# Moving the hi and lo weight tiles, and the activation pairs, to other SBUF addresses

## The chip, the cores and the metric

One core of one Trainium2 chip runs the kernel. The metric is the device time of one execution in microseconds (us), the median of several runs.

## The reference, cut to what matters

One decoder layer for 256 tokens of width 2048, then a final RMSNorm. All inputs are float32.

```
h = h + W_out[ concat( NSA(8 heads), StickBreaking(8 heads) ) ]
h = h + MemoryCrossAttention(rmsnorm(h), rmsnorm(mem))
h = h + PEER(rmsnorm(h))        # s = x U^T for experts, gelu, times V, top-k gated
y = rmsnorm(h)
...
a = jnp.einsum('td,ted->te', xb, u_tab[eb])
hidden = gb.astype(xb.dtype) * jax.nn.gelu(a)
return jnp.einsum('te,ted->td', hidden, v_tab[eb])
```

PEER has 16384 experts, so `u_tab` and `v_tab` have 16384 rows of 2048 numbers each. The kernel computes `x U^T` for all experts, 128 at a time, and multiplies with those rows of V that some token chose.

## The kernel before, in words

Every large product is made with float32r operands in three passes, so that it is nearly as exact as float32. A number is split into `hi` (rounded to float32r by ScalarE) and `lo` (what is left, by VectorE). Of activations both halves lie side by side in a "pair" tile: columns 0 to 255 of a block are the high part of 256 tokens, columns 256 to 511 the low part.

Weights come in pieces of 128x1024 numbers. `raw` (L63) loads a piece through SP's queue into one of four buffers, `parts` (L75) has ScalarE write one of three `hi` buffers (L77) and VectorE one of three `lo` buffers (L79). `scaled` (L110) does the same for rows of V with a factor (L113, L115).

`fm_block` (L152) makes one block of 128 outputs x 256 tokens in two halves of eight 128x128 weight blocks. `fm_mm` (L126) is one half. It issues eight matmuls with a block of `hi` as the stationary operand and 512 columns of the pair as the moving one (L133), and then eight with a block of `lo` and 256 columns (L135). This form carries the projections, W_out (`pair_o`), the memory attention's products, the query product of PEER and all 128 blocks of U (`pair_f`): in all 398 halves, 3184 matmuls at L133 and as many at L135. Stationary blocks are 512 bytes apart in a partition, moving blocks 2048.

`tm_block` (L173) turns the roles round: a block of the pair is stationary, 512 columns of `hi` or `lo` move (L187, L188, L193). `fm_short` (L137) serves the memory attention's output with 256 columns at a time. In the V phase (`v_phase`, products at L1202) a tile of hidden values is stationary (`hh`, `hl`, or a 0/1 tile kept in a `listed` buffer), and 512 columns of `hi` or `lo` of gathered V rows move.

Two smaller products use float32r too. `gates` (L561) splits a 128x384 piece into `wgh` and `wgl` and uses stationary blocks of 24 columns, so 96 bytes apart. `compress` (L508) uses stationary blocks of 60 columns from a tile called `cmp`, 240 bytes apart, against 256 moving columns (L536). `whole_block` (L156) multiplies in plain float32, with the loaded piece as it is (L162).

Tiles get their addresses from pools that are opened one behind the other: constants, then `st` (four `raw`, three `hi`, three `lo`), then `pb` (`pair_x`, `pair_h`, `pair_f`, one after the other in one place), then the front's tiles `fp` (`pair_m`, `pair_o` and `cmp` in one place, `om`), later in its place PEER's `ba` (the gathered rows `hb` and `vrows`) and `gw` (`hh` and `hl`). In the kernel before, the byte address of every `raw`, `hi`, `lo`, pair, `hh` and `hl` is a multiple of 256 (10752 for the first `raw`, 27136 for the first `hi`, 39424 for the first `lo`, 51712 for `pair_f`, 84480 for `pair_o`). So every stationary and every moving operand of L133, L135, L187 to L193 and L1202 starts at the same place modulo 256.

The order of the work is set by the scheduler of the framework and by hand-written dependencies. The program is one stream on each engine, and no instruction reads an address at run time that the change moves, but for the gathers' lists.

Of the kernel before, what the change touches and what calls it, by code (L numbers as in the profile page):

```python
# [18 lines left out]
F32 = mybir.dt.float32  # L19
F32R = mybir.dt.float32r  # L20
# [10 lines left out]
KD = D // 128  # L31
# [3 lines left out]
NEG = -1e30  # L35
N_CMP = 15
HALF = 1024
RAW, HI, LO = 4, 3, 3
GROUP = 8
W = 258  # L40
# [13 lines left out]
class Layer:  # L54
# [18 lines left out]

    def parts(self, raw, eng=None):
        nc = self.nc  # L75
        hi = self.st.tile([128, HALF], F32R, tag="hi", name="hi", bufs=HI)
        self.last_hi = nc.scalar.activation(hi, raw, AF.Copy)  # L77
        lo = self.st.tile([128, HALF], F32R, tag="lo", name="lo", bufs=LO)
        self.last_lo = (eng or nc.vector).tensor_tensor(out=lo, in0=raw, in1=hi.bitcast(F32), op=ALU.subtract)  # L79
        self.pace.append(self.last_lo)  # L80
        self.held()
        return hi, lo

    def split_cut(self, src):

        nc = self.nc
        raw = self.st.tile([128, HALF], F32, tag="raw", name="raw", bufs=RAW)
        hi = self.st.tile([128, HALF], F32R, tag="hi", name="hi", bufs=HI)
        lo = self.st.tile([128, HALF], F32R, tag="lo", name="lo", bufs=LO)
        for n in range(2):  # L90
            cs = slice(n * 512, (n + 1) * 512)
            nc.sync.dma_start(raw[:, cs], src[:, cs])
            nc.scalar.activation(hi[:, cs], raw[:, cs], AF.Copy)
            nc.vector.tensor_tensor(out=lo[:, cs], in0=raw[:, cs], in1=hi[:, cs].bitcast(F32), op=ALU.subtract)
        return hi, lo
# [13 lines left out]

    def scaled(self, raw, val):  # L110
        nc = self.nc
        hi = self.st.tile([128, HALF], F32R, tag="hi", name="hi", bufs=HI)
        nc.scalar.activation(hi, raw, AF.Copy, scale=val)  # L113
        lo = self.st.tile([128, HALF], F32R, tag="lo", name="lo", bufs=LO)
        self.last_lo = nc.vector.scalar_tensor_tensor(lo, raw, val, hi.bitcast(F32), op0=ALU.mult, op1=ALU.subtract)  # L115
        self.held()
        return hi, lo
# [122 lines left out]
    def run(self):  # L240
        nc, tc, a = self.nc, self.tc, self.a
        with ExitStack() as top:
            enter = top.enter_context
            self.accs = ExitStack()
            self.accp = self.accs.enter_context(tc.tile_pool(name="accp", bufs=3, space=bass.MemoryType.PSUM))
            self.cst = enter(tc.tile_pool(name="cst", bufs=1))
            self.dram = enter(tc.tile_pool(name="dram", bufs=1, space=bass.MemoryType.DRAM))
            self.st = enter(tc.tile_pool(name="st", bufs=1))
            self.pb = enter(tc.tile_pool(name="pb", bufs=1))
            c = self.cst  # L250
            self.ident = c.tile([128, 128], F32, name="ident")
            self.iota = c.tile([128, 16], F32, name="iota")
            self.ones = c.tile([128, 128], F32, name="ones")
            self.gs = c.tile([128, 4, KD], F32, name="gs")
            self.rstd = c.tile([128, T], F32, name="rstd")
            self.rstd_c = c.tile([128, 16], F32, name="rstd_c")[:, :2]
            nc.gpsimd.dma_start(self.gs, a["gains"])
            nc.gpsimd.dma_start(self.ident, a["ident"])
            nc.gpsimd.dma_start(self.iota, a["iota"][:, :16])
            nc.vector.memset(self.ones, 1.0)  # L260
            self.hres = self.dram.tile([128, KD, T], F32, name="hres")
            self.rows = [self.dram.tile([n + (hi - lo) * 128, W], F32, name="rows%d" % part)
                         for part, (n, (lo, hi)) in enumerate(zip(ROWS, PARTS))]

            self.table = self.dram.tile([128 * 128 * T, 1], F32, name="table")
            self.by_key = self.table.rearrange("(j x) o -> j (x o)", j=128)
            self.front()
            self.peer()

    def front(self):  # L270
        nc, tc, a = self.nc, self.tc, self.a
        with ExitStack() as es:
            fp = es.enter_context(tc.tile_pool(name="fp", bufs=1))
            ps = es.enter_context(tc.tile_pool(name="fps", bufs=1, space=bass.MemoryType.PSUM))
            self.fp, self.ps = fp, ps
            pair = fp.tile([128, KD, 2 * T], F32R, tag="pair", name="pair_m")
            om = fp.tile([128, 4, 2 * T], F32R, tag="om", name="pair_om")
            self.vt = [fp.tile([128, T], F32, name=n) for n in ("norm_v", "norm_t")]
            self.vt2 = [fp.tile([128, 2], F32, name=n) for n in ("norm_v2", "norm_t2")]
            ssq = fp.tile([128, T], F32, tag="ssq", name="ssq_m")  # L280

            memT = fp.tile([128, KD, T], F32, tag="big", name="memT")
# [88 lines left out]
            for part in range(2):  # L371
                for r in range(0, ROWS[part], 7 * 128):
                    n = min(7, (ROWS[part] - r) // 128)
# [69 lines left out]
            for b2 in range(8):  # L443
                hi, lo = self.split(a["w_mem_o"][b2])
# [116 lines left out]
    def gates(self, xp):  # L561

        nc, a, fp = self.nc, self.a, self.fp
        src = fp.tile([128, KD * 24], F32, tag="l", name="wg", bufs=2)
        nc.sync.dma_start(src, a["w_gate"])
        hi = self.st.tile([128, HALF], F32R, tag="hi", name="wgh", bufs=HI)[:, :KD * 24]
        nc.scalar.activation(hi, src, AF.Copy)
        lo = self.st.tile([128, HALF], F32R, tag="lo", name="wgl", bufs=LO)[:, :KD * 24]
        nc.vector.tensor_tensor(out=lo, in0=src, in1=hi.bitcast(F32), op=ALU.subtract)
        p = self.acc([24, 2 * T])  # L570
        self.fm_mm(p, hi, lo, xp, range(KD), True, True, m=24)
        gT = fp.tile([24, T], F32, name="gT")
        self.join(p, gT)
        nc.vector.tensor_mul(gT, gT, self.rstd[:24, :])
        nc.scalar.activation(gT, gT, AF.Sigmoid)
        p = self.ps.tile([128, 2, 24], F32, tag="sm", name="ps_gt", bufs=1)
        for tb in range(2):
            nc.tensor.transpose(p[:, tb, :], gT[:, tb * 128:(tb + 1) * 128], self.ident[:24, :24])
        out = fp.tile([128, 2, 24], F32, name="gates")
        nc.vector.tensor_copy(out, p)  # L580
        return out
# [136 lines left out]
    def peer(self):  # L718
        nc, tc, a = self.nc, self.tc, self.a
        with ExitStack() as es:  # L720
# [10 lines left out]
            nc.vector.memset(self.unit, 1.0)  # L731
            self.rooms = ba.tile([128, 8], F32, name="rooms")
            nc.gpsimd.dma_start(self.rooms, a["rooms"])
            self.base = ba.tile([128, 40], F32, name="base")[:, :16]
            nc.gpsimd.dma_start(self.base, a["base"])
            self.token = token
            self.listing = False
# [16 lines left out]
            with ExitStack() as e2:  # L754
# [15 lines left out]
                with tc.tile_pool(name="tk", bufs=1, reuse_waits="tile") as tk:  # L770
# [35 lines left out]
                    c = 0  # L806
# [586 lines left out]
    def rest(self, hidden_pair, products, reopen, again):  # L1393
# [3 lines left out]
        count = nc.values_load(self.flag[0:1, 0:1], min_val=0, max_val=16384)  # L1397
        with tc.If(count > 0):
            reopen()
            order = self.st.tile([128, HALF], F32R, tag="lo", name="order", bufs=LO).bitcast(F32)[:, :128]  # L1400
            nc.sync.dma_start(order, a["order"])
            for part, (lo, hi) in enumerate(PARTS):
                n = hi - lo
# [124 lines left out]
```

## Time and profile before

| | |
|---|---|
| time, median of 3 runs | 1696.03 us (1691.76 to 1697.72) |
| the profiled execution's own time | 1684.47 us |
| its span, first to last instruction | 1682.7 us |
| TensorE matmul busy | 1620.0 us, 96% |
| TensorE weight load busy | 1376.6 us, 82% |
| VectorE busy | 1262.5 us, 75% |
| ScalarE busy | 1001.5 us, 60% |
| GpSimd busy | 748.3 us, 44% |
| mean granted TensorE clock | 0.991 |

In the profile a matmul's duration holds its latency, and the next one starts before it has ended, so the durations overlap. How fast matmuls follow each other is read from the distance of their starts, in the timeline; how far one was held up shows in its own duration.

### The profile page before, as it was taken

To read this page: it belongs to the slowest core of one execution; us is meant where nothing else is said; L and a number is where in the kernel's file an instruction comes from. 1 tells how busy PE (TensorE), PEld (TensorE's weight loads), DVE (VectorE), ACT (ScalarE), POOL (GpSimd) and SP (SyncE) were. 2 spreads that over 40 slices of the span, in tenths; PEclk is the share of its full clock that TensorE was granted. 3 is DMA by queue.
4 is the path that set the end of the run, shared out by engine and by line. 5 is a ranking of instruction groups with operands and counts; after the bars stand their busy time and mean duration, and the time that the engine had idled before them with its cause. 6 is when DMAs were issued, how large, how long until landed. Compare 5 with 4: busy or idle time off the path is not lost. (4 is left out here: it accounts for less than half of the span.)

```text
span 1682.7 us, 25655 instructions
## 1 busy us (share of the span) xinstructions
PE 1620.0 (96%) x8760; PEld 1376.6 (82%) x8760; DVE 1262.5 (75%) x2265; ACT 1001.5 (60%) x1486; POOL 748.3 (44%) x656
## 2 busy tenths in 40 slices
PE   8999999999999999999999999999999979989996
PEld 6878777888889888888888878878888858767884
DVE  6876575555668998999999648878665578868687
ACT  6645556775566656666656436665555457656576
POOL 5420000211305266667788761102776318887630
PEclk9999999999999999999999999999999999999998
DMA  8768435789956756666656648876998958998991
GB/s 291 240 200 285 132 119 180 285 319 355 353 179 217 254 178 188 181 188 187 184 178 191 192 150 278 301 258 226 276 271 260 366 191 337 393 372 307 420 411 65
DMA packets 119884, 418.82 MB, mean 249 GB/s; under 512 B 22713, under 2 KB 34633, under 8 KB 106048
## 3 DMA queue, kind: packets, MB, share of 16 engines
q1 hardware_dynamic: 79632, 252.41, 46.5%
q0 software_dynamic: 39824, 164.16, 26.4%
q8 instruction: 70, 1.15, 0.3%
q14 instruction: 70, 0.57, 0.1%
q10 hardware_dynamic: 288, 0.52, 0.1%
HBM read 373.16 MB, written 51.75 MB: 253 GB/s over the span
## 5 line engine op out<-in xcount | busy, mean ns | idle before, releaser
L79 DVE TENSOR_TENSOR lo<-raw,hi 128x1024 fp32r<-128x1024 f32 x437 | 541.2, 1243 | 210.7 <-ACT hi L77 189.5
L77 ACT ACTIVATE hi<-raw 128x1024 fp32r<-128x1024 f32 x437 | 459.4, 1055 | 358.9 <-issue 145.7
L133 PE MATMUL acc<-pair_f,hi 128*128 128x512 f32 x2288 | 576.8, 394 | 6.1 <-ACT hi L77 6.1
L133 PEld LDWEIGHTS acc<-pair_f,hi 128*128 128x128 f32 x2288 | 412.4, 189 | 82.1 <-ACT hi L77 7.9
L1119 POOL DMA_INDIRECT table<-total,place x256 | 312.0, 1219 | 139.7 <-DVE lo L79 63.3
L135 PEld LDWEIGHTS acc<-pair_f,lo 128*128 128x128 f32 x2288 | 311.6, 191 | 30.8 <-DVE lo L79 9.3
L135 PE MATMUL acc<-pair_f,lo 128*128 128x256 f32 x2288 | 320.3, 283 | 7.0 <-DVE lo L79 7.0
L996 POOL DMA_INDIRECT rows<-hb,where x128 | 155.8, 1217 | 47.2 <-issue 28.9
L1173 POOL DMA_INDIRECT vrows<-V,index x88 | 125.9, 1430 | 112.2 <-issue 38.4
L115 DVE SCALAR_TENSOR_TENSOR lo<-vrows,val,hi 128x1024 fp32r<-128x1024 f32 x96 | 122.3, 1281 | 44.6 <-ACT hi L113 35.8
L113 ACT ACTIVATE hi<-vrows,val 128x1024 fp32r<-128x1024 f32 x96 | 108.6, 1146 | 74.4 <-PE out L1202 26.6
L133 PE MATMUL acc<-pair_x,hi 128*128 128x512 f32 x512 | 131.6, 395 | 2.0 <-ACT hi L77 2.0
L133 PEld LDWEIGHTS acc<-pair_x,hi 128*128 128x128 f32 x512 | 91.3, 189 | 18.8 <-ACT hi L77 2.4
L79 DVE TENSOR_TENSOR lo<-vrows,hi 128x1024 fp32r<-128x1024 f32 x80 | 97.3, 1219 | 8.7 <-PE out L1202 3.1
L77 ACT ACTIVATE hi<-vrows 128x1024 fp32r<-128x1024 f32 x80 | 84.0, 1052 | 24.2 <-PE out L1202 13.9
L1202 PE MATMUL out<-hi,hh 128*128 128x512 f32 x256 | 79.9, 406 | 2.3 <-ACT hi L77 1.5
L1202 PE MATMUL out<-hi,hl 128*128 128x512 f32 x256 | 81.1, 402 | 0.8 <-DVE hl L1211 0.5
L1202 PE MATMUL out<-lo,hh 128*128 128x512 f32 x256 | 75.2, 397 | 6.1 <-DVE lo L79 5.9
L135 PEld LDWEIGHTS acc<-pair_x,lo 128*128 128x128 f32 x512 | 70.1, 190 | 7.8 <-DVE lo L79 3.0
L135 PE MATMUL acc<-pair_x,lo 128*128 128x256 f32 x512 | 74.7, 285 | 1.8 <-DVE lo L79 1.7
L133 PE MATMUL acc<-pair_o,hi 128*128 128x512 f32 x256 | 65.2, 394 | 2.4 <-ACT hi L77 1.4
L1202 PE MATMUL out<-hi,listed 128*128 128x512 f32 x192 | 58.0, 398 | 7.5 <-ACT hi L113 7.4
(401 smaller groups left out, 2182.6 us busy)
## 6 DMA issues: line engine op xcount, KB each, us to landing
raw<-U SPq DMA_DIRECT2D x256, 512.0 KB, 4.3
raw<-w_sb SPq DMA_DIRECT2D x32, 512.0 KB, 4.5
table<-zero POOLq DMA_DIRECT2D x16, 1024.0 KB
raw<-w_out SPq DMA_DIRECT2D x32, 512.0 KB, 6.7
raw<-w_pq SPq DMA_DIRECT2D x32, 512.0 KB, 4.3
listed<-rows SPq DMA_DIRECT2D x88, 128.0 KB, 7.5
rows<-zero POOLq DMA_DIRECT2D x12, 903.0 KB
gates<-table POOLq DMA_DIRECT2D x20, 512.0 KB
```

What stands on the lines that cost most here:

```text
L77: self.last_hi = nc.scalar.activation(hi, raw, AF.Copy)
L79: self.last_lo = (eng or nc.vector).tensor_tensor(out=lo, in0=raw, in1=hi.bitcast(F32), op=ALU.subtract)
L113: nc.scalar.activation(hi, raw, AF.Copy, scale=val)
L115: self.last_lo = nc.vector.scalar_tensor_tensor(lo, raw, val, hi.bitcast(F32), op0=ALU.mult, op1=ALU.subtract)
L133: mm(ps, hi[:, n * m:(n + 1) * m], pair[:, k, :], start=first and n == 0, stop=False)
L135: self.last_mm = mm(ps[:, T:], lo[:, n * m:(n + 1) * m], pair[:, k, :T], start=False, stop=last and n == len(ks) - 1)
L996: ins = nc.gpsimd.indirect_dma_start(out=self.rows[part], out_offset=bass.IndirectOffsetOnAxis(ap=where[:, i - lo:i - lo + 1], axis=0), in ...
L1119: ins = self.nc.gpsimd.indirect_dma_start(out=self.table, out_offset=bass.IndirectOffsetOnAxis(ap=self.place[tb][:, s:s + 1], axis=0), in_ ...
L1173: self.gather = nc.gpsimd.indirect_dma_start(out=raw, out_offset=None, in_=self.a["V"], in_offset=bass.IndirectOffsetOnAxis(ap=self.index[ ...
L1202: self.last_mm = mm(out[tb][hf * 2 + q], h, v[:, q * 512:(q + 1) * 512], start=first and n == 0, stop=last and n == len(passes) - 1)
```

## The change

Only addresses change. `hi` and `lo` tiles get 8 columns (32 bytes) more than they use, so that the three buffers of each lie 4128 bytes apart and not 4096. The `lo` buffers move to a pool of their own, `sl`, and a pool `gap` with two small tiles lies between, so that `lo` number j stands at the same address as `hi` number j modulo 256. Two small tiles of the front move ahead of its pair, and `base` is cut from 40 to 24 columns, which moves what lies behind.

```
+PAD = 8
...
-        hi = self.st.tile([128, HALF], F32R, tag="hi", name="hi", bufs=HI)
+        hi = self.st.tile([128, HALF + PAD], F32R, tag="hi", name="hi", bufs=HI)[:, :HALF]
         self.last_hi = nc.scalar.activation(hi, raw, AF.Copy)
-        lo = self.st.tile([128, HALF], F32R, tag="lo", name="lo", bufs=LO)
+        lo = self.sl.tile([128, HALF + PAD], F32R, tag="lo", name="lo", bufs=LO)[:, :HALF]
...
             self.st = enter(tc.tile_pool(name="st", bufs=1))
+            gap = enter(tc.tile_pool(name="gap", bufs=1))
+            self.iota = gap.tile([128, 16], F32, name="iota")
+            self.rstd_c = gap.tile([128, 24], F32, name="rstd_c")[:, :2]
+            self.sl = enter(tc.tile_pool(name="sl", bufs=1))
             self.pb = enter(tc.tile_pool(name="pb", bufs=1))
             c = self.cst
             self.ident = c.tile([128, 128], F32, name="ident")
-            self.iota = c.tile([128, 16], F32, name="iota")
...
-            self.rstd_c = c.tile([128, 16], F32, name="rstd_c")[:, :2]
...
             self.fp, self.ps = fp, ps
+            self.vt2 = [fp.tile([128, 16], F32, name=n)[:, :2] for n in ("norm_v2", "norm_t2")]
             pair = fp.tile([128, KD, 2 * T], F32R, tag="pair", name="pair_m")
             om = fp.tile([128, 4, 2 * T], F32R, tag="om", name="pair_om")
             self.vt = [fp.tile([128, T], F32, name=n) for n in ("norm_v", "norm_t")]
-            self.vt2 = [fp.tile([128, 2], F32, name=n) for n in ("norm_v2", "norm_t2")]
...
-            self.base = ba.tile([128, 40], F32, name="base")[:, :16]
+            self.base = ba.tile([128, 24], F32, name="base")[:, :16]
```

`split_cut`, `scaled`, the gates' `wgh` and `wgl` and a tile of the overflow branch get the same two lines as `parts`. The byte addresses in a partition that come out, modulo 256:

| tile | before | after |
|---|---|---|
| `raw`, four buffers | 0, 0, 0, 0 | 128, 128, 128, 128 |
| `hi`, three buffers | 0, 0, 0 | 128, 160, 192 |
| `lo`, three buffers | 0, 0, 0 | 128, 160, 192 |
| `pair_x`, `pair_h`, `pair_f` | 0 | 224 |
| `pair_m`, `pair_o`, `cmp`, `om` | 0 | 96 |
| `hh`, `hl`, two buffers each | 0, 0 | 160, 160 |
| `vrows`, `hb`, first four buffers | 0, 64, 128, 192 | 160, 224, 32, 96 |
| `whole` | 128 | 32 |

The order of the instructions on every engine stays as it was. Two sets of waits move. In PEER's first blocks the tile `q` is written by ScalarE (L168 before, L169 after) and then by VectorE. The tiles called `q` lie where the front's tile of zeros lay, which DMAs have read. ScalarE's stream at that place, before:

```order
L77 ACTIVATE hi<-raw 128x1024 [waits DMAHW3_49,PE_49,Activation_49]
L168 ACTIVATE q<-acc 128x256 [waits PE_49]
L77 ACTIVATE hi<-raw 128x1024 [waits DMAHW4_49,PE_49,Activation_49]
L1034 ACTIVATE s<-ps_s,rstd_c 128x256 [waits DVE_49,PE_49]
L77 ACTIVATE hi<-raw 128x1024 [waits DMAHW5_49,PE_49,Activation_49]
L786 ACTIVATE whole<-whole,gs 128x256 [waits DMASW0_49]
L786 ACTIVATE whole<-whole,gs 128x256 x3
L168 ACTIVATE q<-acc 128x256 [waits DMASW4_49,DMASW5_49,DMASW3_49,DMASW6_49,DMASW2_49,DMASW7_49,DMASW1_49,PE_49]
```

and now:

```order
L78 ACTIVATE hi<-raw 128x1024 [waits DMAHW3_49,PE_49,Activation_49]
L169 ACTIVATE q<-acc 128x256 [waits DMASW4_49,DMASW3_49,DMASW5_49,DMASW2_49,DMASW6_49,DMASW1_49,DMASW7_49,DMASW0_49,PE_49]
L78 ACTIVATE hi<-raw 128x1024 [waits DMAHW4_49,PE_49,Activation_49]
L1037 ACTIVATE s<-ps_s,rstd_c 128x256 [waits DVE_49,PE_49]
L78 ACTIVATE hi<-raw 128x1024 [waits DMAHW5_49,PE_49,Activation_49]
L789 ACTIVATE whole<-whole,gs 128x256 [waits DMASW0_49]
L789 ACTIVATE whole<-whole,gs 128x256 x3
L169 ACTIVATE q<-acc 128x256 [waits PE_49]
```

The wait for the DMAs that read the zeros (DMASW) goes from the fourth `q` to the third, since the third now overlaps the tile of zeros by 96 bytes. All else stands in the same rows.

More of the change, by code (lines that the diff above doesn't have):

```diff
@@ L87, in split_cut @@
         raw = self.st.tile([128, HALF], F32, tag="raw", name="raw", bufs=RAW)
-        hi = self.st.tile([128, HALF], F32R, tag="hi", name="hi", bufs=HI)
-        lo = self.st.tile([128, HALF], F32R, tag="lo", name="lo", bufs=LO)
+        hi = self.st.tile([128, HALF + PAD], F32R, tag="hi", name="hi", bufs=HI)[:, :HALF]
+        lo = self.sl.tile([128, HALF + PAD], F32R, tag="lo", name="lo", bufs=LO)[:, :HALF]
         for n in range(2):
@@ L111, in scaled @@
         nc = self.nc
-        hi = self.st.tile([128, HALF], F32R, tag="hi", name="hi", bufs=HI)
+        hi = self.st.tile([128, HALF + PAD], F32R, tag="hi", name="hi", bufs=HI)[:, :HALF]
         nc.scalar.activation(hi, raw, AF.Copy, scale=val)
-        lo = self.st.tile([128, HALF], F32R, tag="lo", name="lo", bufs=LO)
+        lo = self.sl.tile([128, HALF + PAD], F32R, tag="lo", name="lo", bufs=LO)[:, :HALF]
         self.last_lo = nc.vector.scalar_tensor_tensor(lo, raw, val, hi.bitcast(F32), op0=ALU.mult, op1=ALU.subtract)
@@ L565, in gates @@
         nc.sync.dma_start(src, a["w_gate"])
-        hi = self.st.tile([128, HALF], F32R, tag="hi", name="wgh", bufs=HI)[:, :KD * 24]
+        hi = self.st.tile([128, HALF + PAD], F32R, tag="hi", name="wgh", bufs=HI)[:, :KD * 24]
         nc.scalar.activation(hi, src, AF.Copy)
-        lo = self.st.tile([128, HALF], F32R, tag="lo", name="wgl", bufs=LO)[:, :KD * 24]
+        lo = self.sl.tile([128, HALF + PAD], F32R, tag="lo", name="wgl", bufs=LO)[:, :KD * 24]
         nc.vector.tensor_tensor(out=lo, in0=src, in1=hi.bitcast(F32), op=ALU.subtract)
@@ L1399, in rest @@
             reopen()
-            order = self.st.tile([128, HALF], F32R, tag="lo", name="order", bufs=LO).bitcast(F32)[:, :128]
+            order = self.sl.tile([128, HALF + PAD], F32R, tag="lo", name="order", bufs=LO).bitcast(F32)[:, :128]
             nc.sync.dma_start(order, a["order"])
```

## Prediction

> **What bounds the kernel now.** I read the page's engine rows first, then the stretches by stage, then single matmuls in the timeline. The page's first part and the stretches (columns: stretch, its length, PE, PEld, DVE, ACT and POOL busy with counts, granted clock, DMA share, GB/s):
>
> ```profile
> PE 1620.0 (96%) x8760; PEld 1376.6 (82%) x8760; DVE 1262.5 (75%) x2265; ACT 1001.5 (60%) x1486; POOL 748.3 (44%) x656
> ...
> 310.00:520.00 210.00, 206.66 (x1211) 181.22 (x1210) 131.59 (x203) 132.56 (x196) 39.34 (x51) 1.00 0.83 298
> ...
> 600.00:1000.00 400.00, 400.00 (x2303) 352.67 (x2302) 345.50 (x810) 234.13 (x346) 295.93 (x242) 1.00 0.62 185
> 1000.00:1360.00 360.00, 346.93 (x1968) 301.52 (x1967) 253.14 (x355) 199.16 (x310) 131.18 (x131) 1.00 0.82 270
> 1360.00:1683.00 323.00, 288.63 (x1240) 225.66 (x1238) 254.14 (x381) 205.97 (x244) 181.87 (x129) 0.96 0.83 317
> ```
>
> Up to 1360 us matmuls run with hardly a gap: 100% of the 400 us in the middle, 98% of W_out's stage (206.66 of 210), 96% from 1000 on. No other engine and no DMA is near its end there. Only the V phase, the last 323 us, waits (89% busy). So time is won or lost by how closely matmuls follow each other, and the change can touch that alone: the order of every engine is the same.
>
> How closely they follow stands in PE's timeline, here in the blocks of U (start, length, what). Start to start counts:
>
> ```profile
> 902.76 2.00 PE L133 MATMUL acc<-pair_f,hi 128*128 128x512 f32 x8
> 904.60 1.11 PE L135 MATMUL acc<-pair_f,lo 128*128 128x256 f32 x8
> 905.55 2.00 PE L133 MATMUL acc<-pair_f,hi 128*128 128x512 f32 x8
> ...
> 913.93 3.82 PE L133 MATMUL acc<-pair_f,hi 128*128 128x512 f32 x16
> 917.59 2.08 PE L135 MATMUL acc<-pair_f,lo 128*128 128x256 f32 x16
> 919.50 2.00 PE L133 MATMUL acc<-pair_f,hi 128*128 128x512 f32 x8
> ```
>
> Eight hi matmuls take 1.84 us (902.76 to 904.60), 230 ns each, and eight lo 0.95 us, 119 ns each: 2.79 us a half, and 398 halves make 1110 us, two thirds of the span. What would a matmul take that nothing held up? The V phase shows it where the clock was halved (the third row is the stretch around the first two, with a granted clock of 0.50; the last three are at full clock):
>
> ```profile
> 1465.16 1.05 PE L1202 MATMUL out<-hi,hl 128*128 128x512 f32 x2
> 1466.01 1.03 PE L1202 MATMUL out<-lo,listed 128*128 128x512 f32 x2
> ...
> 1463.50:1466.80 3.30, 3.30 (x8) 2.15 (x7) 3.28 (x3) 3.21 (x4) 2.96 (x2) 0.50 1.01 409
> ...
> 1446.73 0.61 PE L1202 MATMUL out<-hi,hl 128*128 128x512 f32 x2
> 1447.18 0.62 PE L1202 MATMUL out<-hi,hh 128*128 128x512 f32 x2
> 1447.63 0.62 PE L1202 MATMUL out<-hi,hl 128*128 128x512 f32 x2
> ```
>
> Two take 0.85 us at half clock, 425 ns each, so 512 columns are worth 213 ns at full clock and 256 columns 106 ns. At full clock the V phase spends 227 ns (0.455 for two), 14 more; U's hi 17 more, its lo 13 more. At full speed something holds the operands back. Plain float32 is free of it: 31 steps in 6.7 us, 216 ns for 256 columns, is twice 106 and little besides, at half the columns per time.
>
> ```profile
> L162 PE MATMUL acc<-whole,raw x32: 379/379/382, 613.9 to 620.6; 128*128 128x256 f32 x32
> ```
>
> Whether addresses have a hand in it, two small products can show, for their stationary blocks step through SBUF by 96 bytes (24 columns) and by 240 (60 columns), while all else starts at 0 modulo 256:
>
> ```profile
> 184.08 3.84 PE L133 MATMUL acc<-pair_x,wgh 128*24 128x512 f32 x16
> 187.76 2.01 PE L135 MATMUL acc<-pair_x,wgl 128*24 128x256 f32 x16
> 189.61 0.61 PE L613 MATMUL ps_l<-k_slc,qT 128*128 128x128 f32 x4
> ...
> 113.11 1.10 PE L536 MATMUL ps_hid<-cmp 128*60 128x256 f32 x8
> 114.05 1.31 PE L133 MATMUL acc<-pair_x,hi 128*128 128x512 f32 x5
> ...
> L133 PE MATMUL acc<-pair_x,wgh x16: 388/392/397, 184.1 to 187.5; 128*24 128x512 f32 x16
> L135 PE MATMUL acc<-pair_x,wgl x16: 276/278/281, 187.8 to 189.5; 128*24 128x256 f32 x16
> L536 PE MATMUL ps_hid<-cmp x64: 274/279/285, 113.1 to 160.6; 128*60 128x256 f32 x64
> L133 PE MATMUL acc<-pair_f,hi x2288: 387/393/628, 527.4 to 1359.6; 128*128 128x512 f32 x191
> L135 PE MATMUL acc<-pair_f,lo x2288: 274/283/468, 529.3 to 1360.6; 128*128 128x256 f32 x191
> ```
>
> With 256 columns they follow at 115.6 ns (1.85/16) and 117.5 ns (0.94/8), against 119 when all is aligned, and the middle durations agree: 278 and 279 against 283. With 512 columns `wgh` needs 230 ns (3.68/16), as aligned ones do in a half, and its durations spread from 388 to 397. So the start matters by a few ns a matmul, for better and for worse. They load narrower blocks too, which may be all of the gain.
>
> **The change part by part.** *Lo matmuls, 3184.* They get stationary starts 32, 64 or 96 bytes (modulo 128) from the moving start. The nearest rows for such starts are the two above: 119 − 117.5 = 1.5 ns and 119 − 115.6 = 3.4 ns less. I take the middle, 2.4 ns: 3184 × 2.4 = 7.7 us less. Bounds: the smallest duration of the lo row, 274 against 283, is 9 ns or 28.7 us less; the largest of `cmp`, 285, is 2 ns or 6.4 us more.
>
> *Hi matmuls, 3184.* In the chain of 16 the first eight can be taken at 1.84 us as in every half, which leaves 3.66 − 1.84 = 1.82 for the rest, 227.5 ns each: after lo matmuls some settling of about 2.5 ns a matmul is paid, and it ends when hi follows hi. The new layout shifts the next half by 32 bytes, so the settling changes; `wgh`, with shifting starts, says 230 ns, no change, and the V phase's 227 says 3 ns less. I take a third of that, 1 ns: 3.2 us less. Bounds: 3 ns less (9.6 us), and 397 against 393, `wgh`'s worst duration, 4 ns more (12.7 us).
>
> *V phase.* Its moving operand is `hi` or `lo`, its stationary one starts 32 bytes off either way or not at all. It follows at 227 ns, the least that 512 columns show at full clock here. I count nothing. It can lose: `hh`'s row has 389 in the middle, `wgh`'s has 397 at worst, 8 ns more. On 1152 matmuls (three rows of 256 with `hh` and `hl`, two of 192 with a listed tile) that is 9.2 us, of which only the stretches without waits would count.
>
> ```profile
> L1202 PE MATMUL out<-hi,hh x256: 387/389/796, 1361.6 to 1666.0; 128*128 128x512 f32 x128
> L1202 PE MATMUL out<-lo,hh x256: 387/389/632, 1363.5 to 1667.5; 128*128 128x512 f32 x128
> ...
> L1202 PE MATMUL out<-lo,listed 128*128 128x512 f32 x192 | 61.5, 406 | 3.7 <-DVE lo L115 3.6
> ```
>
> *`tm_block` and `fm_short`*, 384 and 192 matmuls: a tenth of the others, inside the bounds.
>
> *ScalarE and VectorE.* Rows of V lie at 0, 64, 128 and 192 modulo 256 already, `raw` at 0, and the split costs the same:
>
> ```profile
> L79 DVE TENSOR_TENSOR lo<-raw,hi 128x1024 fp32r<-128x1024 f32 x437 | 541.2, 1243 | 210.7 <-ACT hi L77 189.5 <-PE acc L135 10.6 <-ACT eT L626 5.1
> L79 DVE TENSOR_TENSOR lo<-vrows,hi 128x1024 fp32r<-128x1024 f32 x80 | 97.3, 1219 | 8.7 <-PE out L1202 3.1 <-issue 2.7 <-ACT hi L77 1.4
> L77 ACT ACTIVATE hi<-vrows 128x1024 fp32r<-128x1024 f32 x80 | 84.0, 1052 | 24.2 <-PE out L1202 13.9 <-DVE lo L79 4.5 <-DMA vrows<-V,index 2.9
> L77 ACT ACTIVATE hi<-raw 128x1024 fp32r<-128x1024 f32 x437 | 459.4, 1055 | 358.9 <-issue 145.7 <-PE acc L133 107.8 <-DMA raw<-U 37.2
> ```
>
> 1243 against 1219 ns and 1055 against 1052: nothing to lose that PE would see, since both engines wait for PE more than PE for them.
>
> *DMA.* The gathered rows go to starts that are 32 off a multiple of 64; no large transfer of before does. The V phase moves 317 GB/s; if its gathers slowed by 2%, its 323 us could grow by at most 6 us. I take zero, as the transfers' lengths are the same, and keep 6 us for the range.
>
> *The moved wait.* The third `q` (ScalarE, 545.32 us) now waits for DMAs that read the zeros; the last was issued at 460.8 us, 84 us earlier:
>
> ```profile
> L379 POOL DMA_DIRECT2D rows<-zero x14: 532/534/570, 396.7 to 460.8; - x14
> 545.32 0.37 ACT L168 ACTIVATE q<-acc 128x256 f32<-128x256 f32 x1
> ```
>
> Nothing is held up by it. If those DMAs were late, ScalarE's next `hi` and so PE would wait behind it; 84 us are the cover.
>
> *Sum.* 7.7 + 3.2 = 10.9 us less; PE is busy 96 to 100% of those stages, and of the rest faster matmuls only make waits longer, so 10 us. The profiled execution took 1684.47 us; it would take 1674.5. The runs' median is 1696.03, 11.6 us more than the profiled execution; the same 10 us taken from it give 1686.0 us.
>
> Two pages bear on it. The Trainium skill's "SBUF — State Buffer", section "Who interferes with whom", gives TensorE independent read ports for the moving operand and for weight loads, and says that PE never waits on anyone; by that the sum would be zero (a rival below). The 388 and 397 of `wgh`, alike but for their stationary starts, speak against it. The skill's "TensorE: Matmul & The Clock Gate", section "Back-to-back issue gap", gives N/2.4 + 2.5 ns for an isolated pair at full clock, 216 and 109 ns; an estimate by it is 14 + 10 ns to win on each pair, 76 us in all. No full-clock float32r row here comes near it, so it sets no bound of mine.
>
> **The rivals.**
>
> *Addresses do not matter (0.20).* The 14 ns would be TensorE's own at this rate, and the narrow blocks the reason for 115.6 and 117.5. For it: the V phase and U's chain settle at the same 227 ns. Then 1696 us.
>
> *No chain settles: slower (0.30).* Now every half starts 32 bytes from the last, against one fixed relation before; the calm 389 to 393 ns may be the fruit of that one relation. `wgh`, whose relation changes with each matmul, has durations up to 397. If hi goes to 397 (12.7 us), lo stays, and the V phase loses a third of its 9.2 us, that is 16 us: 1712 us. The turning point is where hi loses more than the 2.4 ns that lo gains. Against it: within a half all eight starts are alike, as before.
>
> *All is won (0.10).* Lo falls to its row's least, 274 (28.7 us), hi stays: 1668 us.
>
> **How the numbers follow.** My forecast, 1686.0 us, has 0.40. A measurement of this kernel can tell about 0.3%, 5 us, from no change. Faster by more: 0.40 + 0.10 = 0.50. Same: 0.20. Slower: 0.30. The forecast's own range is 3 to 18 us less. For 8 in 10 the range reaches from the full gain, 1668, to the slow rival, 1712, which leaves out about 1 in 10 at each end.
>
> **What would show it.** In the changed kernel's timeline: eight lo in 0.93 us instead of 0.95, eight hi in 1.83 instead of 1.84, V pairs still at 0.455. Lo's middle duration would be near 279, hi's near 392. Wrong would be: lo at 283 still (addresses do not matter), or hi and `hh` rows with 397 in the middle (slower). Changed lengths at ScalarE or VectorE, or a wait before the third `q`, would be a cause that I have counted at nothing.

## The result, and the profile after

The changed kernel takes 1705.37 us, the median of 7 runs (1702.99 to 1710.31). The kernel before, in 7 runs beside it, takes 1694.93 us (1688.53 to 1700.84). The ratio is 1.0064 with an interval of 1.0046 to 1.0083: slower by 10.4 us, where 10 us less had been forecast. A second timing, 12 runs against 23, gave 1694.70 against 1690.93 us, ratio 1.0022 (1.0001 to 1.0042). Both say slower, by 3.8 and by 10.4 us; the two intervals do not meet, so how much is not settled.

The two profiled executions are further apart than that, 1684.47 and 1710.31 us, because the one of before was faster than all seven of its runs and the one of the change the slowest of its own. What the 26 us hold besides the change comes further down. First the page of the changed kernel (its lines have moved by one at `parts` and `fm_mm`, by three in the V phase):

```profile
PE 1640.7 (96%) x8760; PEld 1376.8 (81%) x8760; DVE 1260.7 (74%) x2265; ACT 1002.0 (59%) x1486; POOL 766.0 (45%) x656
...
L80 DVE TENSOR_TENSOR lo<-raw,hi 128x1024 fp32r<-128x1024 f32 x437 | 541.2, 1243 | 239.4 <-ACT hi L78 127.7
L78 ACT ACTIVATE hi<-raw 128x1024 fp32r<-128x1024 f32 x437 | 459.7, 1056 | 348.1 <-issue 141.4
...
L80 DVE TENSOR_TENSOR lo<-vrows,hi 128x1024 fp32r<-128x1024 f32 x80 | 97.4, 1221 | 10.7 <-PE out L1205 5.8
L78 ACT ACTIVATE hi<-vrows 128x1024 fp32r<-128x1024 f32 x80 | 84.0, 1052 | 26.8 <-PE out L1205 13.8
```

VectorE and ScalarE do their work as before, to 2 ns an instruction (1243 and 1243, 1055 and 1056, 1219 and 1221, 1052 and 1052). PE is busier, by 20.7 us with the same 8760 matmuls (POOL, busy for 45%, too, by 17.7 us). Where, the single matmuls tell (durations in ns, min/median/max):

```profile
L134 PE MATMUL acc<-pair_f,hi x2288: 387/396/784, 531.2 to 1380.2; 128*128 128x512 f32 x191
L136 PE MATMUL acc<-pair_f,lo x2288: 274/279/580, 533.1 to 1381.3; 128*128 128x256 f32 x191
L1205 PE MATMUL out<-hi,hh x256: 387/395/795, 1382.3 to 1691.8; 128*128 128x512 f32 x128
L1205 PE MATMUL out<-lo,hh x256: 387/395/796, 1384.2 to 1693.3; 128*128 128x512 f32 x128
```

Lo went from 283 to 279, just as forecast. Hi went from 393 to 396, where 392 had been forecast, and the V phase from 389 to 395. In the timeline the starts show what that makes of a half (start, length):

```profile
899.20 2.03 PE L134 MATMUL acc<-pair_f,hi 128*128 128x512 f32 x8
901.06 1.10 PE L136 MATMUL acc<-pair_f,lo 128*128 128x256 f32 x8
902.00 2.02 PE L134 MATMUL acc<-pair_f,hi 128*128 128x512 f32 x8
903.87 1.12 PE L136 MATMUL acc<-pair_f,lo 128*128 128x256 f32 x8
904.82 2.03 PE L134 MATMUL acc<-pair_f,hi 128*128 128x512 f32 x8
906.69 1.10 PE L136 MATMUL acc<-pair_f,lo 128*128 128x256 f32 x8
907.62 2.03 PE L134 MATMUL acc<-pair_f,hi 128*128 128x512 f32 x8
```

Three halves, one for each of the three buffers, take 907.62 − 899.20 = 8.42 us, 2807 ns each against 2793. Eight hi take 1.86 or 1.87 us (1.84 before), eight lo 0.93 to 0.95 (0.95 before). Over all recorded pairs of neighbours hi follows hi at 232.6 ns (230.1 before) and lo follows lo at 118.0 (119.0 before): 8 × 2.5 − 8 × 1.0 = 12 ns more a half, and 398 halves make 4.8 us.

The stretches, cut as before:

```profile
310.00:520.00 210.00, 206.68 (x1197) 179.32 (x1196) 129.59 (x200) 131.75 (x195) 40.02 (x52) 1.00 0.82 298
600.00:1000.00 400.00, 391.93 (x2205) 339.32 (x2204) 338.73 (x816) 226.28 (x334) 307.07 (x235) 0.98 0.59 177
1000.00:1360.00 360.00, 353.70 (x2002) 305.85 (x2001) 249.46 (x348) 198.62 (x307) 143.38 (x139) 0.99 0.81 263
```

W_out's stage is as busy as before (206.68 of 210 us) and gets 1197 matmuls done, not 1211 (1205 in the later trace of before). But the 400 us in the middle hold something else: PE is not busy there for 8 us. Nearly all of it is one place. The same 20 us of the changed kernel and of the kernel before:

```profile
950.00:970.00 20.00, 13.13 (x40) 8.92 (x39) 5.05 (x6) 4.44 (x7) 12.80 (x12) 0.70 0.15 45
```

```profile
950.00:970.00 20.00, 20.00 (x117) 17.64 (x116) 9.90 (x11) 9.87 (x15) 15.52 (x15) 1.00 0.68 187
```

40 matmuls in place of 117, and the DMA share falls from 0.68 to 0.15 with them. The timeline of the changed kernel shows PE loading a weight block only every 0.71 us and VectorE standing for 12 us, while POOL goes on:

```profile
956.70 0.98 POOL L1122 DMA_INDIRECT table<-total,place  x1 [0.30 <-issue]
957.22 0.19 PEld L134 LDWEIGHTS acc<-pair_f,hi 128*128 128x128 f32 x1 [0.30 <-issue]
957.93 0.29 PEld L134 LDWEIGHTS acc<-pair_f,hi 128*128 128x128 f32 x1 [0.53 <-issue]
958.64 0.29 PEld L134 LDWEIGHTS acc<-pair_f,hi 128*128 128x128 f32 x1 [0.42 <-issue]
966.51 2.40 DVE L80 TENSOR_TENSOR lo<-raw,hi 128x1024 fp32r<-128x1024 f32 x2 [11.92 <-issue]
```

"issue" means that the engine waits for nothing that the profile shows. The lost matmuls are worth some 13 us (77 of 117 × 20 us). Whether the change makes this stretch is the first question below. The stage lengths in the two traces differ by 3.7 us up to W_out, 16.6 in U's blocks (these 13 us in it, against a stall of 4 us near 1005 us in the trace of before) and 5.2 in the V phase.

### The profile page after: what moved, and what is told of

The parts are those of the page before. It is cut to its first block, busy times and chain, and to the rows that moved or that the text cites. A ratio compares the mean times of both kernels' runs of the same rounds, so it can differ in the third digit from the quotient of the medians.

```text
span 1708.5 us, 25656 instructions
## 1 busy us (share of the span) xinstructions
PE 1640.7 (96%) x8760; PEld 1376.8 (81%) x8760; DVE 1260.7 (74%) x2265; ACT 1002.0 (59%) x1486; POOL 766.0 (45%) x656
## 5 line engine op out<-in xcount | busy, mean ns | idle before, releaser
L80 DVE TENSOR_TENSOR lo<-raw,hi 128x1024 fp32r<-128x1024 f32 x437 | 541.2, 1243 | 239.4 <-ACT hi L78 127.7
L78 ACT ACTIVATE hi<-raw 128x1024 fp32r<-128x1024 f32 x437 | 459.7, 1056 | 348.1 <-issue 141.4
L134 PE MATMUL acc<-pair_f,hi 128*128 128x512 f32 x2288 | 586.4, 398 | 12.0 <-issue 6.2
L1122 POOL DMA_INDIRECT table<-total,place x256 | 329.8, 1288 | 134.9 <-issue 59.4
L999 POOL DMA_INDIRECT rows<-hb,where x128 | 159.4, 1245 | 52.7 <-issue 32.9
L1176 POOL DMA_INDIRECT vrows<-V,index x88 | 122.2, 1389 | 115.6 <-issue 37.5
L80 DVE TENSOR_TENSOR lo<-vrows,hi 128x1024 fp32r<-128x1024 f32 x80 | 97.4, 1221 | 10.7 <-PE out L1205 5.8
L78 ACT ACTIVATE hi<-vrows 128x1024 fp32r<-128x1024 f32 x80 | 84.0, 1052 | 26.8 <-PE out L1205 13.8
```

Of the source, the lines that this page charges most:

```text
L134: mm(ps, hi[:, n * m:(n + 1) * m], pair[:, k, :], start=first and n == 0, stop=False)
L999: ins = nc.gpsimd.indirect_dma_start(out=self.rows[part], out_offset=bass.IndirectOffsetOnAxis(ap=where[:, i - lo:i - lo + 1], axis=0), in ...
L1122: ins = self.nc.gpsimd.indirect_dma_start(out=self.table, out_offset=bass.IndirectOffsetOnAxis(ap=self.place[tb][:, s:s + 1], axis=0), in_ ...
L1176: self.gather = nc.gpsimd.indirect_dma_start(out=raw, out_offset=None, in_=self.a["V"], in_offset=bass.IndirectOffsetOnAxis(ap=self.index[ ...
```

## The experiments

*Place* is my theory after the result: how closely matmuls follow each other depends on the distance, weights' start minus pair's start modulo 256, and each distance has its price. Before, it is 0 everywhere; after, it is 160, 192 and 224 (that is −96, −64 and −32) by buffer, and 32, 64 and 96 at the front's pair. The main rival, *hop*, is the forecast's "No chain settles": what costs is that each half has another distance than the last. A third is that absolute addresses count.

**The change again, and the kernel before again**, with no edit.

> The changed kernel once more, one look. Its first profile has a stretch from 950 to 970 us in which all engines stand and PE issues 40 matmuls where the kernel before issues 117. 'Hiccup' (the stretch is an event of single executions and no part of what the change does): a second profile has no such stretch at that place or has it elsewhere, and its U stage after the table is shorter than 763.3 us by about 13 us, near 750. 'Part of it' (the change makes it): the stretch comes again within some us of 950 us and the stage is 763 us again. By the spacings alone (12 ns a half x 398, 5 ns x 384 of the table's block, V hidden) the time is 5 to 8 us over the kernel before.

> The kernel before once more, one look. Its first profile has one stall of 4 us near 1005 us and none at 950 us. 'Hiccup': the same kernel can show the stretch of standing engines too, or another time near the median of its own runs, 1692 to 1697 us, with the U stage after the table some us longer than 746.7 us. 'Part of the change': no such stretch, the stage within 2 us of 746.7 us.

The changed kernel took 1699.01 us this time, with a U stage of 752.6 us; the kernel before took 1692.78, also with 752.6. The row of the kernel before for the 20 us:

```profile
950.00:970.00 20.00, 16.96 (x76) 12.88 (x74) 5.56 (x6) 5.62 (x8) 15.65 (x15) 0.91 0.37 106
```

The kernel before can be held up there too: 76 matmuls, not 117. So the change does not make this stretch (nor does the granted clock of 0.70 in its first row: the changed kernel's two later profiles have 1.00 there, with 81 and 75 matmuls), and some 9 us of the difference between the first two profiles (13 against 4) fall away. The rate of matmuls beside it does not vary like that: from 600 to 940 us both traces of before hold 1960 matmuls, and those of the changed kernel 1948 here and 1949 in the second timing, 0.6% fewer (1939 in its first trace, where PE also stands for 1 us in that row). I read the U stage by that row from here on. The stage's whole length does not show the loss here: the 6.2 us between these two runs lie 3.7 us before U's blocks and 2.5 us in the V phase.

**A sweep of the distance.** All that is left of the kernel is the chains: 24 hi matmuls, 24 lo, and halves of 8 and 8, at 16 distances, with nothing to wait for. The decoder's computation is left out.

```
OFFS = [o * STEP for o in range(16)]
...
        for o in OFFS:
            hi_both(o, hi, lo, w, w0, o == 0)
        for _ in range(4):
            for o in (40, 48, 56):
                hi(w, o, False)
                lo(w, o, False)
...
    hi(w, o, first, 24)
    lo(w, o, False, 24)
    for _ in range(3):
        hi(w, o, False)
        lo(w, o, False)
...
```

`hi` issues eight matmuls of 512 columns (24 where it says so), `lo` of 256; `o` counts columns of four bytes, so 40, 48 and 56 are the change's 160, 192 and 224 bytes.

> This kernel computes nothing of the reference: it runs chains of hi matmuls (512 columns) and lo matmuls (256 columns) alone, one operand moved from the other in steps of 16 bytes, and its output is a filler. Per step: 24 hi, 24 lo, three times eight hi and eight lo at the same start, then three times eight hi at distance 0 and eight lo at the step. Theory 'place' (a matmul's spacing is set by the distance of its own two operands): the chains of 24 hi give 227 ns at distance 0 and about 233 ns at most others, constant in a chain; lo gives 120 ns at 0 and 115 to 119 ns elsewhere. Theory 'hop' (only a change of the distance from half to half costs): all chains of 24 hi settle at 227 ns whatever the distance, and only the stretch that goes round three distances shows 233. Rival 'absolute' (a start off a multiple of 64 costs, whatever the other operand): the second sweep, with the moving operand 32 bytes on, is slower throughout.

Distances 0, 160 and 192 in the sweep's timeline:

```profile
31.50 2.00 PE L35 MATMUL acc<-pair,w 128*128 128x512 f32 x8
33.34 1.11 PE L40 MATMUL acc<-pair,w 128*128 128x256 f32 x8
34.30 2.00 PE L35 MATMUL acc<-pair,w 128*128 128x512 f32 x8
...
283.85 2.03 PE L35 MATMUL acc<-pair,w 128*128 128x512 f32 x8
285.72 1.12 PE L40 MATMUL acc<-pair,w 128*128 128x256 f32 x8
286.68 2.03 PE L35 MATMUL acc<-pair,w 128*128 128x512 f32 x8
...
334.10 1.99 PE L35 MATMUL acc<-pair,w 128*128 128x512 f32 x8
335.93 1.11 PE L40 MATMUL acc<-pair,w 128*128 128x256 f32 x8
336.87 2.00 PE L35 MATMUL acc<-pair,w 128*128 128x512 f32 x8
```

Halves of 2.80, 2.83 and 2.77 us, from nothing but the start of the weights. Worked out to the ns (the last 16 of each chain of 24, the last two of three halves), twelve of the sixteen distances:

| distance | 0 | 16 | 32 | 64 | 96 | 144 | 160 | 176 | 192 | 208 | 224 | 240 |
|---|---|---|---|---|---|---|---|---|---|---|---|---|
| hi after hi, long chain, ns | 226.7 | 233.3 | 233.4 | 233.5 | 234.3 | 233.1 | 233.3 | 229.6 | 228.9 | 232.0 | 233.3 | 226.7 |
| lo after lo, long chain, ns | 120.0 | 118.2 | 118.5 | 117.7 | 117.3 | 120.1 | 120.2 | 118.1 | 117.7 | 116.6 | 116.7 | 117.3 |
| half of 8 hi and 8 lo, ns | 2794 | 2760 | 2816 | 2780 | 2808 | 2828 | 2827 | 2796 | 2756 | 2785 | 2801 | 2777 |

Distance 0 gives the kernel's own half, 2794 against 2793. It is the best hi there is in a long chain and among the worst lo; most other starts cost hi 5 to 8 ns. With the pair moved on by 32 bytes and the weights too, a half takes 2792 ns, and the seven other starts tried there agree within 10 ns with the halves of the same distance at the pair's first place: for a half's time absolute addresses fall, the distance counts. That it counts modulo 256 shows in distance 0 itself: the sweep's weights lie 20736 bytes behind its pair, an odd multiple of 256, the kernel's first `hi` 24576 ahead of `pair_f`, an even one, and the halves take the same. Going round 160, 192 and 224 as the change does, halves take 2825, 2781 and 2804 ns, 2803 in the mean; held at one distance they take 2827, 2756 and 2801. So there is a hop as well, and it takes from the good middle one only, 25 ns.

**All pairs 96 bytes on, the weights as before**: distance 160 throughout, no hop.

```
+            enter(tc.tile_pool(name="gap", bufs=1)).tile([128, 24], F32, name="gap")
             self.pb = enter(tc.tile_pool(name="pb", bufs=1))
...
-            self.base = ba.tile([128, 40], F32, name="base")[:, :16]
+            self.base = ba.tile([128, 80], F32, name="base")[:, :16]
```

> The kernel before with all pairs 96 bytes on; hi, lo, hh and hl stay at 0 modulo 256, so the distance is the same -96 in every half. 'place': hi at 233 ns and lo at about 119 instead of 230 and 119 on average, 8 x 3 ns x 398 halves = 9.6 us slower than before, about 1704 us where before is 1695. 'hop': nothing changes from half to half, hi settles at 227 as before, lo stays at 120: no change, 1695 us.

Measured: 1696.81 against 1689.02 us, ratio 1.0031 (1.0007 to 1.0055). Hi follows at 233.1 ns and lo at 120.1, as in the sweep:

```profile
905.67 2.03 PE L133 MATMUL acc<-pair_f,hi 128*128 128x512 f32 x8
907.54 1.12 PE L135 MATMUL acc<-pair_f,lo 128*128 128x256 f32 x8
908.50 2.03 PE L133 MATMUL acc<-pair_f,hi 128*128 128x512 f32 x8
```

Slower without any hop: as the only cause the hop falls. The size, 5 us by the ratio (1 to 9 by its interval), is less than the 33 ns × 398 = 13 us that the halves ask for; that shortfall stays unexplained.

**All pairs 64 bytes on**, the same edit with 16 and 88 columns: distance 192 throughout.

> The kernel before with all pairs 64 bytes on, everything else at its place: the distance is -64 in every half. The sweep gives 2756 ns a half there, against 2794 at 0 and 2827 at -96. 398 x 38 ns = 15.1 us less; tm_block, where the roles are turned, gets 384 x 6.8 = 2.6 us more: about 12 us faster than before if nothing hides it (1677 where before is 1689). 'hop' (only hops from half to half cost): no change. If waits elsewhere take back what PE gains, as pairs96 lost 5 to 8 us where the sweep gave 13: 5 to 8 us faster.

Measured: 1672.30 against 1681.56 us, ratio 0.9952 (0.9935 to 0.9970). This one is faster than both kernels. The second timing, together with the changed kernel's:

> The constant -64 kernel (the kernel before with all pairs 64 bytes on) a second time, beside the changed kernel. Its first ratio, 0.9952, was taken where the kernel before ran 1681.6 us and no profile had the stretch of standing engines near 950 us; the kernel with lo at distance +64 got 0.9966 where the kernel before ran 1693.1 us and its profile had that stretch. 'Place' alone: ratio again 0.994 to 0.997, whatever the session. 'Saturated': the same, and lo at +64 is no better than this. 'Session': the gain of a cheaper half is smaller where the standing stretch comes (above 0.997), since what PE gives up there waits anyway.

> The changed kernel a second time, timed beside the constant -64 kernel on one chip. Spacings as in its two profiles (halves 12 ns above 2793 ns). By the halves and the table's block alone (12 ns x 398 + 5 ns x 384 = 6.7 us, the V phase hidden): ratio 1.004. With the V phase's 4.8 ns x 1152 = 5.5 us counting too: 1.007. If the standing stretch near 950 us were part of the change and not of the session, its profile would have 13 us there that the constant -64 kernel's profile of the same call has not, and the ratio would be 1.007 or more.

1684.47 for distance 192 and 1694.70 for the change, against 1690.93 us: ratios 0.9966 (0.9945 to 0.9987) and 1.0022 (1.0001 to 1.0042). Both kernels are held up at 950 us in these profiles (66 and 75 matmuls in the 20 us), which again takes the stretch off the change. Halves at distance 192, in the first profile:

```profile
897.24 1.99 PE L133 MATMUL acc<-pair_f,hi 128*128 128x512 f32 x8
899.07 1.11 PE L135 MATMUL acc<-pair_f,lo 128*128 128x256 f32 x8
900.01 2.00 PE L133 MATMUL acc<-pair_f,hi 128*128 128x512 f32 x8
901.85 1.07 PE L135 MATMUL acc<-pair_f,lo 128*128 128x256 f32 x8
902.76 1.99 PE L133 MATMUL acc<-pair_f,hi 128*128 128x512 f32 x8
```

2.77 and 2.75 us in turn. The rate from 600 to 940 us shows the order without the noise of the runs: the kernel before, the change (second timing), distance 160, distance 192.

```profile
600.00:940.00 340.00, 340.00 (x1960) 299.86 (x1959) 316.68 (x779) 205.78 (x304) 250.07 (x200) 1.00 0.62 185
```

```profile
600.00:940.00 340.00, 340.00 (x1949) 297.17 (x1949) 316.45 (x780) 205.87 (x303) 256.88 (x200) 1.00 0.61 184
```

```profile
600.00:940.00 340.00, 340.00 (x1939) 297.05 (x1938) 315.59 (x795) 204.53 (x301) 245.75 (x198) 1.00 0.61 182
```

```profile
600.00:940.00 340.00, 340.00 (x1983) 299.93 (x1982) 317.07 (x777) 207.48 (x306) 256.12 (x201) 1.00 0.60 187
```

1.2% more matmuls at 192, 0.6% fewer in the change, 1.1% fewer at 160. At 192 that is worth 9 us of U's 747; the runs got 8.1 and 5.7 by their ratios. In the traces W_out and what lies between it and U win 2 us more, and the V phase gives 3 back: 325.7 and 325.1 us against 322.0 and 322.4, with its matmuls' spacing unchanged at 227.8 ns. It begins earlier and waits longer.

**The changed kernel without its hop**: everything as in the change, but spacing 4096, all hi and lo buffers at the place of the middle one (distance 192 to U's pair, 64 at the front's, 0 to `hh`).

```
-PAD = 8
+PAD = 0
...
+            enter(tc.tile_pool(name="gap1", bufs=1)).tile([128, 8], F32, name="gap1")
+            self.sh = enter(tc.tile_pool(name="sh", bufs=1))
...
-            self.rstd_c = gap.tile([128, 24], F32, name="rstd_c")[:, :2]
+            self.rstd_c = gap.tile([128, 48], F32, name="rstd_c")[:, :2]
             self.sl = enter(tc.tile_pool(name="sl", bufs=1))
+            enter(tc.tile_pool(name="gap2", bufs=1)).tile([128, 16], F32, name="gap2")
```

> The changed kernel with its three hi and three lo buffers 4096 bytes apart again, all at 160 modulo 256, the place of its middle one: -64 to the activations' pair and +64 to the front's, hh and hl at distance 0; all else lies as in the change. If the hop from half to half and the two outer distances are the loss: 2756 ns for 358 halves and 2780 for 40, 14 us less than before, tm_block 2 us more: about 12 us faster than before and over 20 faster than the change. If anything else of the change costs (the targets of the DMAs, the split's operands, the moved wait): it stays near 1705 or between.

Measured: 1674.87 against 1681.56 us, ratio 0.9964 (0.9949 to 0.9980), and the spacings are those of distance 192 again, 229.2 and 116.1 ns.

```profile
L134 PE MATMUL acc<-pair_f,hi x2288: 387/392/659, 529.8 to 1350.5; 128*128 128x512 f32 x191
L136 PE MATMUL acc<-pair_f,lo x2288: 275/279/469, 531.6 to 1351.5; 128*128 128x256 f32 x191
```

So the places of `raw`, `vrows`, `hb`, `whole` and the moved waits cost nothing that shows; the change loses by its spacing of 4128 bytes, which brings both the hop and the two outer distances. In the change, with the hop, the matmuls of the same middle buffer follow at 231.7 and 117.5 ns: 8 × (2.5 + 1.4) = 31 ns more a half.

**4128 with the pairs left at 0**: distances 0, 32 and 64.

```
+PAD = 8
...
+            enter(tc.tile_pool(name="gap", bufs=1)).tile([128, 40], F32, name="gap")
+            self.sl = enter(tc.tile_pool(name="sl", bufs=1))
+            enter(tc.tile_pool(name="gap2", bufs=1)).tile([128, 40], F32, name="gap2")
```

> The kernel before with hi and lo buffers 4128 bytes apart (0, 32 and 64 modulo 256) and the pairs, hh and hl at 0: the distance hops from half to half and is 0 in every third. 'hop': as slow as the change or slower, 1705 us. 'place': a third of the halves at distance 0 keep 230 or better, the others get 233, and lo gets 119, 118 and 115: about 3 us slower than before, 1698 us.

Measured: 1693.98 against 1689.02 us, ratio 1.0020 (0.9998 to 1.0042). Hi follows at 230.2, 232.7 and 232.9 ns, lo at 118.5, 118.2 and 115.0: the mean half is as long as before. Whether this kernel is slower at all stays open.

**`hh` and `hl` 32 bytes on**, and the gathered rows with them; all else as before (`base` 48 columns wide).

> The kernel before with everything behind base moved by 32 bytes: hh, hl and the gathered rows, so only the V phase's distances (32) and the DMAs' targets (32 off a multiple of 64) change. If the V phase carries a share of the loss: 5 ns on 1152 matmuls, up to 5.8 us slower, about 1700 us, spacing 233 in place of 227. If its waits for gathered rows hide it: within 2 us of before. If the DMAs' targets cost: gathers land later, and the V phase grows by more than 6 us.

```profile
L1202 PE MATMUL out<-hi,hh x256: 389/395/796, 1366.0 to 1672.7; 128*128 128x512 f32 x128
L1202 PE MATMUL out<-lo,hh x256: 388/395/792, 1367.9 to 1674.2; 128*128 128x512 f32 x128
```

The V phase's matmuls get as long as in the change, 395 in the middle, and the time does not move: 1690.82 against 1689.02 us, ratio 0.9993 (0.9971 to 1.0015). Some 5 ns on the 768 matmuls with `hh` and `hl` would make 3.8 us, and the interval allows 2.5 at most, so a part of it at least is hidden. The phase's other waits are the likely cover; which of them was not looked for.

**Hi's distance and lo's apart**: a grid of 16 × 16 in the manner of the sweep (the computation is left out here too).

```
for oh in OFFS:
    for ol in OFFS:
        for _ in range(3):
            hi(w, oh, first)
            lo(w2, ol, False)
            first = False
```

> Computes nothing of the reference: chains of eight hi and eight lo alone, as in the first sweep, three times for each of 16 x 16 pairs of distances (hi's and lo's, in steps of 16 bytes); its output is a filler. 'place' (each matmul pays for the distance of its own operands alone): the time of a half is the sum of a hi part that depends on hi's distance and a lo part that depends on lo's, so the best half is the best hi row (about 227 x 8) with the best lo column (114 to 117 x 8), 2740 ns or less. Rival 'meeting' (what counts is also how hi's last matmuls and lo's first meet): the times are no such sum, as the first sweep's 2756 at -64 and at 16 for both suggest, where hi alone takes 229 and 233.

256 cells from 2746 to 2833 ns, 2801 in the mean. The cheapest are hi at 192 with lo at 64 (2746), 240 with 192 (2754), 192 with 192 (2756) and 0 with 208 (2760). 0 with 0 is at 2793, cheaper than the mean cell. Row means and column means leave a rest of 8 ns (standard deviation) beside 10 and 7 for rows and columns: the two distances do not simply add up. Fifteen of the sixteen cells with one distance for both agree with the first sweep within 10 ns; 16 with 16 does not. It takes 2812 ns here and took 2760 there, with hi following at 233 and at 227 ns. So the distance alone does not settle a half's time everywhere, and what else does was not tried.

**The cheapest cell in the kernel**: lo in a pool of its own, 128 bytes on, and the pairs 64 on.

```
+            enter(tc.tile_pool(name="gap", bufs=1)).tile([128, 32], F32, name="gap")
+            self.sl = enter(tc.tile_pool(name="sl", bufs=1))
+            enter(tc.tile_pool(name="gap2", bufs=1)).tile([128, 48], F32, name="gap2")
...
-            self.base = ba.tile([128, 40], F32, name="base")[:, :16]
+            self.base = ba.tile([128, 88], F32, name="base")[:, :16]
```

> The kernel before with the lo tiles 128 bytes on (a pool of their own, same 4096-byte spacing) and the pairs 64 bytes on: distance weights minus pair is 192 for hi and 64 for lo everywhere but in the V phase (hi at 0, lo at 128). The grid's cheapest cell is just this one, 2746 ns a half, against 2756 for 192 and 192 and 2793 for 0 and 0. The constant -64 kernel got 8.1 us of the (2793 - 2756) x 398 halves = 14.7 us that the sweep gives for it, a share of 0.55. 'Place' (the two distances set the half's time, the kernel keeps about that share): hi near 229 ns, lo near 114 to 115, and (2793 - 2746) x 398 x 0.55 = 10.3 us below the kernel before, ratio 0.994 (0.992 to 0.996 by the interval of that share). 'Saturated' (what is left over in the constant -64 kernel already waits for another engine, so a shorter half buys nothing more): spacings as above but ratio 0.995 or more. 'V counts after all' (lo at 128 makes the V phase's halves slower and the table and V stages lose what the U stage wins): V's lo spacing above 118 and its stage longer than 325.7 us by over 2 us, ratio 0.996 or more.

```profile
600.00:940.00 340.00, 340.00 (x1989) 299.44 (x1988) 316.51 (x779) 207.72 (x305) 270.32 (x202) 1.00 0.63 188
```

Hi at 229.2 and lo at 114.9 ns as the grid has it, and 1.5% more matmuls in the stretch than before. Yet the time is 1686.28 against 1693.14 us, ratio 0.9966 (0.9948 to 0.9984), no better than with distance 192 for both. That lies where the expectation put "saturated", but the waiting engine was not found; its V phase, 323.5 us, is no longer than that of distance 192. And 10 ns a half more are 4 us at most, 0.24%, hardly more than the interval's half width of 0.18%. Whether the gain was hidden or only too small to see stays open.

## Why the prediction was wrong, step by step

*What bounds the kernel.* Right. The same program, with 31 to 40 ns less a half, runs 0.3 to 0.5% faster, and with 12 to 33 more runs slower; the one other cost that shows is small (2 us in `tm_block`, below).

*Lo, 7.7 us less.* Right in sign, too large: 1.0 ns a matmul, 3184 × 1.0 = 3.2 us (the forecast's own product, 3184 × 2.4, is 7.6). The two rows that I had taken the middle of, `wgl` and `cmp`, have stationary blocks of 24 and 60 columns; the sweep, with blocks of 128, has lo between 116.7 and 120.2 ns at the buffers' three distances.

*Hi, 3.2 us less.* This is the step that failed. I had read U's chain of 16, which comes down from 230 to 227.5 ns, as a settling that any constant start reaches, and took a third of the V phase's 3 ns as a gain. The sweep shows that in long chains 226.7 is the value of distance 0 and of 240 alone, and that 160 and 224, where two of three buffers were put, cost 233. The kernel was at hi's best place. Instead of 1 ns less it became 2.5 more, 3184 × 2.5 = 8.0 us. `wgh`'s durations up to 397, which stood in my own quoted row, were the better guide, and I used them as a bound only.

*`tm_block` and `fm_short`, inside the bounds.* Too easy: `tm_block`'s 384 matmuls went from 228 to about 233 ns, 2 us. It shows in the stretch from 160 to 310 us, 751 and 750 matmuls in the change, 747 and 751 at distance 192, and 758 in both traces of before.

*The V phase, nothing.* Right by luck in part. Its spacing rose from 227.7 to between 230.8 and 233.1 ns, up to 5.5 us on 1152 matmuls, and `hh` 32 bytes on alone shows most of such a rise without a loss that can be seen.

*VectorE, ScalarE, DMA, nothing.* Right: durations equal to 2 ns, and the changed kernel without its hop, which keeps all those places, wins. *The moved wait, nothing.* Right: `q` starts at 549.18 us, the last DMA that reads the zeros was issued at 464.2.

```profile
548.22 1.06 ACT L78 ACTIVATE hi<-raw 128x1024 fp32r<-128x1024 f32 x1 [0.85 <-ACT norm_t L208]
549.18 0.36 ACT L169 ACTIVATE q<-acc 128x256 f32<-128x256 f32 x1
```

```profile
L382 POOL DMA_DIRECT2D rows<-zero x14: 532/534/570, 400.6 to 464.2; - x14
```

*The sum.* With the measured sizes: 8.0 − 3.2 + 2 = 6.8 us more, between the two timings' 3.8 and 10.4.

*The rivals.* "Addresses do not matter" falls with the sweep (2756 to 2828 ns from the same instructions) and with distance 192. "All is won" does not exist at these distances. "No chain settles" named the result's sign and its turning point, hi losing more than lo wins, and its sign, 397 ns in the middle, was nearly met (396 for hi, 395 for `hh`); its mechanism is half of it. Without a hop the three distances cost 2826 ns (the kernel at 160), 2762 (at 192) and 2801 (sweep, 224), 2796 in the mean against 2793: the two outer places eat what the middle one wins. The hop then takes the middle one's 31 ns, on a third of the halves, 4.1 us.

*The pages.* The Trainium skill's "SBUF — State Buffer", section "Who interferes with whom", gives PE independent read ports for the moving operand and for weight loads, and says that PE never waits on anyone. As a forecast of no change this failed: with no other engine at work, a half takes from 2756 to 2828 ns by the distance between the two operands. Where inside PE or on the way to it the time goes, no run shows. The gap of an isolated matmul in the Trainium skill's "TensorE: Matmul & The Clock Gate", section "Back-to-back issue gap", 216 and 109 ns by estimate, was met at no distance: the closest means of long chains are 226.7 and 113.3.

## What to carry to other kernels

Before moving tiles, measure the chain by itself at the starts in question; one short kernel prices them all, and the place that looks crowded (all at 0) can be better than the mean. Expect the kernel to keep only a part of such a price: at distance 192 the halves promised 31 ns × 398 = 12 us, and the runs got 8.1 and 5.7. Read two operands' addresses as a distance and price the large and the small matmuls apart, since they want different places. Keep that distance the same from one buffer to the next: a spacing that shifts it costs a good place part of its gain.

## What the runs showed of the hardware that was not expected

- With float32r operands, how closely matmuls follow depends on the distance of the stationary operand's start from the moving one's modulo 256: 226.7 to 234.3 ns for 512 columns, 116.6 to 120.2 for 256, in the long chains of the first sweep. Long lo chains at distances 64 and 192 took 117.7 there and 113.3 with pair and weights both 32 bytes on, while their halves agreed to 4 ns; why was not tried. Buffers that lie 4096 bytes apart behave alike.
- At distance 0 eight hi after eight lo begin at 233.5 and 235.5 ns and come down to 226.5 from the sixth on. At 160 they go 232, 238, 231 in turn and never come down.
- Near 950 us PE, VectorE and ScalarE can fall to a third or a half of their work in 20 us, in waits for nothing that the profile shows ("issue") and with the DMA share down to 0.15, in the kernel before too; it is worth up to 13 us. Three of the twelve profiles of full kernels do not show it at that place. Two of these come from one chip, where the kernel before ran at 1681.6 us; all eight profiles from three other chips, where it ran at 1689.0 to 1693.1 us, show it, some of them weakly. What sets it off was not tried; two profiles should not be compared before it is taken out.
